# The last two chunks of the first feed-forward: four and four feature tiles become two and six, and the last chunk's down weights are split into other buffers

## The chip, the cores and the metric

The kernel runs on one core of one Trainium2 chip. The metric is the time of one execution in device microseconds (us). All operands are 32-bit; products are computed in three passes on numbers split into a high and a low part.

## The reference, cut to what matters

One decoder layer on 512 tokens of width 1024. Three sub-layers follow each other, each between two RMS norms:

```python
h = h + 0.5 * rmsnorm(swiglu(rmsnorm(h, ffn1_pre_w), ffn1_w_gu, ffn1_w_down), ffn1_post_w)
u = rmsnorm(h, mix_pre_w)
h = h + rmsnorm(token_mixing(u, mem, w_in, ...), mix_post_w)
h = h + 0.5 * rmsnorm(swiglu(rmsnorm(h, ffn2_pre_w), ffn2_w_gu, ffn2_w_down), ffn2_post_w)

def swiglu(x, w_gu, w_down):
    g, u = split(x @ w_gu, 2)          # 1024 x 5632, two halves of 2816
    return (silu(g) * u) @ w_down      # 2816 x 1024
```

The 2816 hidden features are 22 tiles of 128. The token mixing begins with a projection of the normed tokens `u` by parts of `w_in`.

## The kernel before, in words

**Splitting.** A 32-bit operand is split by `split` (L160): ScalarE (ACT) writes the high part (L161), VectorE (DVE) writes the rest (L162, through `tt`, so its rows show L158). A product is then three matmuls: hi by hi, hi by lo, lo by hi. `mm3` (L339) issues them with 512 moving columns (L341 to L343), `product` (L355) with 256 columns (L361 to L363).

**Gate and up.** For the feature tiles 2 to 21 a gate tile and an up tile are computed together as a pair, by seven products instead of eight on quarter blocks of the tokens and the weights (`pair`, L366): products 1, 6, 5, 7, 2, 3, 4 in this order, each of 4 x 3 matmuls of 256 columns. The moving operands of products 1, 2 and 3 are quarters of the split tokens `xhi`/`xlo`. Those of products 4, 5, 6 and 7 are combinations of token quarters, stored split in four tile pairs that the code calls `t4`, `t1`, `t2` and `t3` (`self.xc`, L80, and the table `self.xop`, L83). Each is a high and a low tile of 128 x 4 x 256. They are written by `prenorm` (L234 to L238) for the tokens of the next sub-layer, when the third and the fourth token tile are normed, and are read by every pair until the sub-layer's last pair. The seven weight operands of a pair are split into the pool `w` (18 buffers of 128 x 512, so nine split operands), in the order of the products.

**Down.** The features go in chunks, `CHUNKS1` and `CHUNKS2` (L44, L45): 2, 4, 4, 4, 4, 4 tiles. While the pairs of one chunk are computed, the down projection of the chunk before is woven in: eight accumulations `down` (four token tiles by two column halves, L462), spread over the chunk's pairs (L501). Each has 3 matmuls of 512 columns for each feature tile of the chunk, and ends in one VectorE addition to `y`. Its weights are split into the pool of 37 general buffers `slots` (`down_weights`, L457).

**The last chunk.** It has no pairs to be woven into. Its down weights are loaded row by row of tiles (L508, 512 KB each, into the pool `st` of four buffers) and split at L509: the tiles 0 to 2 into the pool `w`, the fourth (`j >= 3`) into `slots`. Then, for each of the four token tiles (L513), come two accumulations, the second one of the fourth token tile in two parts of 256 columns; squares (L174), the reciprocal root on GpSimd (POOL, L181), the products with the gain, the addition to the residual (`postnorm`, L244). A task is spawned (L527) that norms the token tile for the next sub-layer: squares, reciprocal root, `u` (L190), eight TensorE transposes into PSUM (L196), splits into `xhi`/`xlo` (L217), copies (L208), and the combinations for the third and fourth tile. The task gives way after `u` and is resumed when a count of TensorE time (`tick`, L109) has grown by `LAT['norm'] = 8` us; that sets where its transposes stand in TensorE's instruction stream.

**What follows.** The mixing begins with `values` (L847): eight split weight operands in the pool `w` (`rows`, L274), and four accumulations of 24 matmuls of 512 columns, one for each token tile, each of which needs its token tile normed. Three pairs follow. A scheduler orders each engine's instructions when the kernel is built: it goes by the order in which they were written and by when it takes their operands to be ready. Every engine then runs its list in that order.

The second feed-forward is the same function, with `CHUNKS2`.

Of the kernel before, what the change touches and what calls it, by code (L numbers as in the profile page):

```python
# [40 lines left out]

ORDER = ("hg0", "prep", "v1", "hg1", "v2", "kv", "v0", "dil0", "mq0", "mq1", "dil1", "b_hg", "b_mem", "b_dil")

CHUNKS1 = (2, 4, 4, 4, 4, 4)  # L44
CHUNKS2 = (2, 4, 4, 4, 4, 4)  # L45

LAT = dict(comb=1.0, mem0=0.5, mem1=8.0, mem2=1.5, hg=1.5, hgx=6.0, hg1=6.0, hg2=11.0, hg3=6.0, hg4=6.0, dil0=4.0, dil1=17.0, dil2=5.0,
# [2 lines left out]
HALVES = (slice(0, 512), slice(512, 1024))  # L50


class Layer:
# [193 lines left out]
    def load(self, w, r0, nr, c0, ncol):  # L247

        st = self.stage.tile([P, nr, ncol], F32, tag="st", name=f"st{self.uid()}")
        self.bring(st, w.rearrange("(k p) c -> p k c", p=P)[:, r0:r0 + nr, c0:c0 + ncol])  # L250
        return st

    def unit(self, shape, slot=False):

        if slot:
            return self.slot(shape, F32R)
        return self.wpool.tile(list(shape), F32R, tag="w", name=f"w{self.uid()}")
# [163 lines left out]
    def ffn(self, w_gu, w_down, w_post, ready, reload, after, chunks, early, plain):  # L421
# [63 lines left out]
        f0, before, ws = 0, None, []  # L485
        for n in chunks:
            act = []
            for j in range(n):
                if before and 2 * j % n == 0:
                    ws = []  # L490
# [12 lines left out]
                        down(i % NT, i // NT, before[2], ws, before[0] == 0)  # L503
            before = (f0, n, act)
            f0 += n
        ws = []
        for j in range(n):
            st = self.load(w_down, before[0] + j, 1, 0, D)  # L508
            ws.append([self.wsplit(st[:, 0, HALVES[hf]], j >= 3) for hf in range(2)])  # L509
        h = reload()  # L510
        gain = self.bcast_gain(w_post)
        tasks = []
# [495 lines left out]
def layer_kernel(ctx, tc, a, nbias, hmask, out):  # L1008
# [35 lines left out]
    def reload(src):  # L1044
        def go():
            h = [[L.slot() for _ in range(2)] for _ in range(NT)]
            for t in range(NT):
                for hf in range(2):
                    L.fetch(h[t][hf], src(t, hf))
            return h  # L1050
        return go

    def follow(dest, w):

        gain, raw = [], {}

        def after(h, t):
            if t == 0:
                gain.extend(L.bcast_gain(w))
            for hf in range(2):  # L1060
                nc.sync.dma_start(out=dest[t][hf], in_=h[t][hf])
            return L.prenorm(h[t], gain, t, LAT['norm'], raw)
        return after

    def store(h, t):
        for c, n in ((0, 512), (512, 256), (768, 256)) if t == NT - 1 else ((0, 512), (512, 512)):
# [4 lines left out]
    ready = L.ffn(a["ffn1_w_gu"][0], a["ffn1_w_down"][0], a["ffn1_post_w"][0], [first, second],  # L1071
                  reload(lambda t, hf: x[t * P:(t + 1) * P, HALVES[hf]]), follow(h1, a["mix_pre_w"][0]), CHUNKS1, PLAN['early1'], PLAN['plain1'])
    z = L.mixing(a, ready, nbias)
# [44 lines left out]
```

## Time and profile before

| | us |
|---|---|
| median of 3 runs (lowest to highest) | 1367.3 (1366.92 to 1368.4) |
| the profiled execution | 1367.62 |
| its span, first to last instruction | 1365.8 |
| TensorE busy in it | 1331.6 |
| VectorE busy | 1050.7 |
| ScalarE busy | 742.2 |

The profile is that of one execution, and its times count from the start of the span. Engines are PE (TensorE), PEld (TensorE's weight loads), DVE (VectorE), ACT (ScalarE), POOL (GpSimd) and SP (the queue that issues most DMAs). A row of the timeline has the start, the duration, the engine, the line, the operation, the output and inputs by the program's names, and in square brackets the idle time before the instruction and what ended it. Matmuls overlap: the time that one costs is the distance between two starts, not its duration. Buffers of one pool share a name: `w` is the split-weight pool, `s` the general slots, `st` the staged loads, `ps` and `px` PSUM.

### The profile page before, as it was taken

To read this page: it belongs to the slowest core of one execution; us is meant where nothing else is said; L and a number is where in the kernel's file an instruction comes from. 1 tells how busy PE (TensorE), PEld (TensorE's weight loads), DVE (VectorE), ACT (ScalarE), POOL (GpSimd) and SP (SyncE) were. 2 spreads that over 40 slices of the span, in tenths; PEclk is the share of its full clock that TensorE was granted. 3 is DMA by queue.
4 is the path that set the end of the run, shared out by engine and by line. 5 is a ranking of instruction groups with operands and counts; after the bars stand their busy time and mean duration, and the time that the engine had idled before them with its cause. 6 is when DMAs were issued, how large, how long until landed. Compare 5 with 4: busy or idle time off the path is not lost.

```text
span 1365.8 us, 24324 instructions
## 1 busy us (share of the span) xinstructions
PE 1331.6 (97%) x9197; PEld 1233.0 (90%) x9197; DVE 1050.7 (77%) x1996; ACT 742.2 (54%) x1527; POOL 107.0 (8%) x140
## 2 busy tenths in 40 slices
PE   6999999999999999999999999999999999999997
PEld 6999999999789888899899999999889999999996
DVE  6887776777798975598888988897478877677765
ACT  6665544555467655355554755566366655445541
POOL 1111111110100000000000100000011111111100
PEclk9999999999999999999999999999999999999999
DMA  9676565554435335334224333335465765655513
GB/s 271 141 182 184 148 156 142 143 151 125 168 94 177 96 98 163 123 102 117 63 78 124 100 95 93 108 94 154 135 190 135 186 181 151 152 139 148 146 47 139
DMA packets 238123, 185.76 MB, mean 136 GB/s; under 512 B 9109, under 2 KB 198966, under 8 KB 238006
## 3 DMA queue, kind: packets, MB, share of 16 engines
q1 hardware_dynamic: 224246, 160.02, 39.5%
q0 software_dynamic: 12032, 21.04, 9.4%
q10 hardware_dynamic: 1728, 3.15, 0.6%
q8 instruction: 72, 1.18, 0.3%
q14 instruction: 45, 0.37, 0.1%
HBM read 153.73 MB, written 9.47 MB: 119 GB/s over the span
## 4 chain that ended last, share of the span: by engine, by line
PE 87%; DVE 6%; issue 3%; DMA 2%; ACT 1%; POOL 1%; SPq 0%; POOLq 0%; DVEq 0%; ACTq 0%
PE ps L361 17%; PE ps L363 17%; PE ps L362 17%; PE ps L341 6%; PE ps L342 6%; PE ps L343 6%; PE px L341 5%; PE px L342 5%; PE px L343 5%; PE px L348 4%; DVE s L158 2%; PE px L352 1%; DVE w L158 1%; POOL r L181 1%; DVE s L244 1%
## 5 line engine op out<-in xcount | busy, mean ns | idle before, releaser
L161 ACT ACTIVATE w<-sum 128x512 fp32r<-128x512 f32 x288 | 180.2, 631 | 215.9 <-PE ps L362 180.3
L158 DVE TENSOR_TENSOR w<-sum,w 128x512 fp32r<-128x512 f32 x288 | 196.9, 687 | 76.9 <-ACT w L161 75.9
L361 PE MATMUL ps<-xhi,w 128*128 128x256 f32 x864 | 246.3, 285 | 0.9 <-ACT s L379 0.9
L363 PE MATMUL ps<-xhi,w 128*128 128x256 f32 x864 | 244.8, 283 | 0.0
L362 PE MATMUL ps<-xlo,w 128*128 128x256 f32 x864 | 244.4, 283 | 0.0
L161 ACT ACTIVATE w<-st 128x512 fp32r<-128x512 f32 x260 | 162.9, 630 | 126.7 <-PE ps L362 90.0
L158 DVE TENSOR_TENSOR w<-st,w 128x512 fp32r<-128x512 f32 x260 | 177.2, 688 | 39.3 <-ACT w L161 37.9
L158 DVE TENSOR_TENSOR s<-s,s 128x256 f32<-128x256 f32 (+3 forms) x316 | 176.8, 564 | 16.2 <-ACT s L161 4.6
L361 PEld LDWEIGHTS ps<-xhi,w 128*128 128x128 f32 x864 | 165.6, 192 | 3.8 <-ACT s L379 1.2
L362 PEld LDWEIGHTS ps<-xlo,w 128*128 128x128 f32 x864 | 165.6, 192 | 2.4 <-issue 0.2
L363 PEld LDWEIGHTS ps<-xhi,w 128*128 128x128 f32 x864 | 165.5, 192 | 0.0
L158 DVE TENSOR_TENSOR sum<-sum,st 128x512 f32<-128x512 f32 x176 | 120.4, 687 | 10.9 <-issue 5.0
L158 DVE TENSOR_TENSOR s<-s,ps 128x256 f32<-128x256 f32 (+1 forms) x194 | 92.3, 476 | 29.4 <-PE ps L343 24.0
L341 PE MATMUL px<-s,s 128*128 128x512 f32 x288 | 112.6, 391 | 0.0
L342 PE MATMUL px<-s,s 128*128 128x512 f32 x288 | 112.5, 391 | 0.0
L343 PE MATMUL px<-s,s 128*128 128x512 f32 x288 | 112.0, 389 | 0.0
L361 PE MATMUL ps<-t4hi,w 128*128 128x256 f32 x288 | 81.9, 284 | 0.8 <-ACT s L382 0.8
L361 PE MATMUL ps<-t3hi,w 128*128 128x256 f32 x288 | 82.6, 287 | 0.0
L362 PE MATMUL ps<-t3lo,w 128*128 128x256 f32 x288 | 82.0, 285 | 0.0
L361 PE MATMUL ps<-t1hi,w 128*128 128x256 f32 x288 | 81.7, 284 | 0.0
L363 PE MATMUL ps<-t1hi,w 128*128 128x256 f32 x288 | 81.6, 283 | 0.0
L362 PE MATMUL ps<-t2lo,w 128*128 128x256 f32 x288 | 81.5, 283 | 0.0
(186 smaller groups left out, 3344.2 us busy)
## 6 DMA issues: line engine op xcount, KB each, us to landing
st<-in_ffn_w_gu_dram SPq DMA_DIRECT2D x48, 512.0 KB, 4.9
st<-in_w_in_dram SPq DMA_DIRECT2D x48, 512.0 KB, 3.7
st<-in_ffn_w_down_dram SPq DMA_DIRECT2D x44, 512.0 KB, 3.8
sum<-in_ffn_w_gu_dram SPq DMA_DIRECT2D x80, 256.0 KB, 3.4
sh<-in_ffn_w_gu_dram SPq DMA_DIRECT2D x40, 256.0 KB, 3.8
sum<-sh POOLq DMA_DIRECT2D x40, 256.0 KB, 3.6
sum<-st POOLq DMA_DIRECT2D x40, 256.0 KB, 3.3
sum<-in_w_in_dram SPq DMA_DIRECT2D x32, 256.0 KB, 2.9
```

The lines of the kernel that those rows point to most:

```text
L158: self.pin(self.nc.vector.tensor_tensor(out=out, in0=a, in1=b, op=op))
L161: self.pin(self.nc.scalar.activation(hi, src, AF.Copy))
L181: self.nc.gpsimd.tensor_tensor(out=r, in0=v, in1=self.mhalf[:, :1], op=ALU.pow)
L244: self.nc.vector.scalar_tensor_tensor(out=h[hf][:, cs], in0=y[hf][:, cs], scalar=r, in1=h[hf][:, cs], op0=ALU.mult, op1=ALU.add)
L341: mm(out, lhsT=lhs[0], rhs=rhs[0], start=first, stop=False)
L342: mm(out, lhsT=lhs[0], rhs=rhs[1], start=False, stop=False)
L343: mm(out, lhsT=lhs[1], rhs=rhs[0], start=False, stop=last)
L348: self.nc.tensor.matmul(out, lhsT=lhsT, rhs=rhs, start=start, stop=stop, **k)
L352: self.nc.tensor.transpose(out, in_, self.ident)
L361: mm(out, lhsT=lh, rhs=rh, start=first and k == 0, stop=False, skip_group_check=True)
L362: mm(out, lhsT=lh, rhs=rl, start=False, stop=False, skip_group_check=True)
L363: mm(out, lhsT=ll, rhs=rh, start=False, stop=k == 3, skip_group_check=True)
```

## The change

The chunks of the first feed-forward become 2, 4, 4, 4, 2, 6; those of the second stay. In both, the weights of the last chunk go elsewhere: tiles 0 and 1 into the pool `w` as before, the others into the space of the combinations `t2`, `t1`, `t3`, `t4`, in this order, each cut into two pieces of 128 x 512. With six tiles that is 8 of the 12 split operands, column half 0 in `t2` and `t1`, half 1 in `t3` and `t4`; with four tiles it is 4 of 8, in `t2` and `t1`. None of them go to `slots` any more.

```diff
-CHUNKS1 = (2, 4, 4, 4, 4, 4)
+CHUNKS1 = (2, 4, 4, 4, 2, 6)
 CHUNKS2 = (2, 4, 4, 4, 4, 4)
...
+    def spare(self):
+
+        for n in ("t2", "t1", "t3", "t4"):
+            for j in range(2):
+                yield [x[:, 2 * j:2 * j + 2, :].rearrange("p a b -> p (a b)") for x in self.xc[n]]
...
-        ws = []
+
+        ws, spare = [], list(self.spare())
         for j in range(n):
             st = self.load(w_down, before[0] + j, 1, 0, D)
-            ws.append([self.wsplit(st[:, 0, HALVES[hf]], j >= 3) for hf in range(2)])
+            ws.append([])
+            for hf in range(2):
+                i = j - 2 + (n - 2) * hf
+                if j < 2 or i >= len(spare):
+                    ws[-1].append(self.wsplit(st[:, 0, HALVES[hf]]))
+                else:
+                    self.split(*spare[i], st[:, 0, HALVES[hf]])
+                    ws[-1].append(spare[i])
```

## The prediction

> **What bounds the kernel now.** I read the page first, then the windows around the edited code, then TensorE's waits there and the timeline of each engine.
>
> ```profile
> span 1365.8 us, 24324 instructions
> PE 1331.6 (97%) x9197; PEld 1233.0 (90%) x9197; DVE 1050.7 (77%) x1996; ACT 742.2 (54%) x1527; POOL 107.0 (8%) x140
> PE 87%; DVE 6%; issue 3%; DMA 2%; ACT 1%; POOL 1%; SPq 0%; POOLq 0%; DVEq 0%; ACTq 0%
> ```
>
> TensorE is busy 97% of the span and is 87% of the chain that ended last. So an edit pays only where TensorE stands still. These windows are four pairs of the first feed-forward, its last chunk up to the last down matmul, the values stage, and the three pairs after it:
>
> ```profile
> 193.71:255.87 62.16, 62.16 (x435) 58.33 (x434) 45.94 (x81) 31.08 (x60) 6.98 (x8) 1.00 0.60 152
> 345.50:371.10 25.60, 24.47 (x126) 20.30 (x125) 18.04 (x32) 10.43 (x27) 3.70 (x5) 1.00 0.48 167
> 371.10:398.10 27.00, 24.36 (x113) 19.14 (x112) 25.71 (x48) 18.89 (x41) 2.86 (x5) 1.00 0.32 99
> 398.10:428.30 30.20, 30.20 (x253) 30.20 (x252) 28.04 (x53) 20.66 (x43) 0.00 (x0) 1.00 0.53 152
> ```
>
> The columns are window, length, then busy time and count of PE, PEld, DVE, ACT, POOL, then granted clock and DMA share. Pairs run without a hole; the last chunk and the values stage do not, and in the values stage DVE is busy 25.71 of 27.00 us. TensorE's own starts show each hole:
>
> ```profile
> 345.49 0.39 PE L341 MATMUL ps<-w,s 128*128 128x512 f32 x1
> ...
> 359.54 0.39 PE L343 MATMUL ps<-w,s 128*128 128x512 f32 x1
> 359.84 1.32 PE L352 MATMUL px<-ident,s 128*128 128x128 f32 x8
> 360.92 0.48 PE L341 MATMUL ps<-w,s 128*128 128x512 f32 x1
> ...
> 365.57 0.39 PE L343 MATMUL ps<-s,s 128*128 128x512 f32 x1
> 367.08 0.66 PE L352 MATMUL px<-ident,s 128*128 128x128 f32 x4 [1.13 <-DVE s L190]
> ...
> 370.89 0.40 PE L341 MATMUL ps<-w,xhi 128*128 128x512 f32 x1
> ...
> 373.86 0.39 PE L341 MATMUL ps<-w,xhi 128*128 128x512 f32 x1
> 375.02 0.63 PE L352 MATMUL px<-ident,s 128*128 128x128 f32 x4 [0.77 <-DVE s L190]
> ...
> 378.95 0.39 PE L342 MATMUL ps<-w,xhi 128*128 128x512 f32 x1
> 381.11 0.50 PE L342 MATMUL ps<-w,xhi 128*128 128x512 f32 x1 [1.78 <-DVE w L158]
> ...
> 383.29 0.39 PE L341 MATMUL ps<-w,xhi 128*128 128x512 f32 x1
> 383.74 1.29 PE L352 MATMUL px<-ident,s 128*128 128x128 f32 x8
> ...
> 398.07 0.28 PE L361 MATMUL ps<-xhi,w 128*128 128x256 f32 x1
> ```
>
> From 345.49 to 359.54 there are 62 steps of 512-column matmuls, 14.05/62 = 0.227 us each. A 256-column step is 30.20/253 = 0.119 us. A hole is a start, minus the start before it, minus 0.227: 0.07, 1.28, 0.93, 1.93 and 0.22 us, together 4.43. Three sorts of wait are in them: for `u` (L190) of a token tile that TensorE is to transpose, 0.07 + 1.28 + 0.93 + 0.22 = 2.50; and for a split weight of the values stage, 1.93. The same from above: the last chunk's 84 whole and 24 half-width matmuls, 96 of the values stage and 32 transposes (eight cost 360.92 − 359.84 = 1.08) need 180 x 0.227 + 24 x 0.119 + 4 x 1.08 = 48.0 of the 398.07 − 345.49 = 52.6 us. About 4.5 us is all that the edited place can give.
>
> **Why the holes are there.** A token tile takes TensorE 24 x 0.227 = 5.4 us, and its transposes stand 8 us of TensorE time behind its end. Tile 0 ended at 345.5 + 5.4 = 350.9, tile 1 at 356.4.
>
> ```profile
> 351.13 0.69 DVE L158 TENSOR_TENSOR s<-s,ps 128x512 f32<-128x512 f32 x1 [2.03 <-PE ps L343]
> 353.51 0.69 DVE L158 TENSOR_TENSOR s<-s,s 128x512 f32<-128x512 f32 x1 [0.69 <-DMA s<-in_ffn_post_w_dram]
> ...
> 359.03 1.42 DVE L190 SCALAR_TENSOR_TENSOR s<-s,r,s 128x512 f32<-128x512 f32 x2 [0.44 <-POOL r L181]
> ...
> 361.57 0.20 DVE L180 TENSOR_SCALAR v<-ss,ss 128x1 f32<-128x1 f32 x1
> ...
> 366.28 1.42 DVE L190 SCALAR_TENSOR_TENSOR s<-s,r,s 128x512 f32<-128x512 f32 x2
> ```
>
> Tile 0's chain, alone, has the first half of `u` after 359.84 − 350.9 = 8.9 us, 0.7 of them for a gain that landed late. Tile 1's needs 367.08 − 356.4 = 10.7: its second addition and its `v` (361.57) stand behind tile 0's `u` on DVE. DVE falls behind because four chains of about 7.6 us each (ten steps of 0.6 to 0.7, two of 0.2 and two waits of 0.44 for POOL) meet a period of 5.4.
>
> **The change, part by part.** *A longer period.* With six tiles a token tile takes 36 x 0.227 = 8.2 us. DVE's 7.6 us fit, barely. TensorE reaches the transposes of tile 0 at 8.2 + 0.7 = 8.8 us behind its end, as now, and those of tiles 1 and 2 at 9.9 and 10.2 (eight transposes of the tile before lie between). Readiness is 8.2 to 8.9 alone, plus up to 1.4 for the L190 pair of the tile before: 9.6. So the holes of 1.28 and 0.93 close. For tile 3 nothing about the place changes, 8 us behind, 38 x 0.227 + 1.08 = 9.7; the shortest chain is 8.9 and it still meets tile 2's splits and combinations. I leave 0.8 there (bounds 0.3 and 1.8).
>
> *The pool `w`.* The last chunk held 12 of its 18 buffers, now 8.
>
> ```profile
> 331.46 0.63 ACT L161 ACTIVATE w<-st 128x512 fp32r<-128x512 f32 x1 [4.89 <-PE ps L362]
> ...
> 337.22 0.63 ACT L161 ACTIVATE w<-st 128x512 fp32r<-128x512 f32 x1 [0.55 <-PE ps L362]
> ...
> 340.10 0.63 ACT L161 ACTIVATE w<-st 128x512 fp32r<-128x512 f32 x1 [0.17 <-PE ps L362]
> ...
> 364.90 0.61 ACT L161 ACTIVATE w<-st 128x512 fp32r<-128x512 f32 x1
> ...
> 376.38 0.62 ACT L161 ACTIVATE w<-st 128x512 fp32r<-128x512 f32 x1
> ...
> 380.32 0.61 ACT L161 ACTIVATE w<-st 128x512 fp32r<-128x512 f32 x1
> ```
>
> Now three of the eight operands of the values stage (337.22 to 340.10) are split before the last chunk, into buffers that the last pair gives back; a fourth at 364.9; the rest from 376.38 on, because their buffers hold down weights until the last down matmul at 370.8. In the new order five come from the last pair, a sixth when token tile 3 begins, two near its end. The hole of 1.93 shrinks to about 0.2 (bounds 0 and 1). DVE also loses some 3 x 0.6 us of work from its fullest stretch.
>
> *The new wait.* These rows are the end of the last pair (its next TensorE work starts at 340.02), the low part of its activation, and the first later write of a combination:
>
> ```profile
> 340.02 0.40 PE L341 MATMUL px<-s,s 128*128 128x512 f32 x1
> ...
> 342.14 0.69 DVE L158 TENSOR_TENSOR s<-s,s 128x512 fp32r<-128x512 f32 x1
> ...
> 386.69 0.63 ACT L161 ACTIVATE t1hi<-s 128x512 fp32r<-128x512 f32 x1 [0.51 <-DVE s L158]
> ```
>
> The eight splits into `t2`, `t1`, `t3`, `t4` wait for products 6, 5, 7 and 4 of the last pair. Behind them on ACT stand that pair's copies, silu and split, and DVE's halves wait for ACT. The last pair ends, two short downs follow (12 x 0.227 = 2.7 us), then the last chunk begins with the `w` tiles 0 and 1; half 0 of the last tile is needed 15 x 0.227 = 3.4 us later and comes from `t1`, free two products and more before the end. Half 1 in `t4` is needed 4.1 + 2.7 us in. Slack is over 3 us everywhere; cost nothing. The combinations' next writers come 386.7 − 370.9 = 15.8 us after the last down matmul now, so their wait is hidden too. The other cover is thinner: the gain's DMA, which stands in SP's order behind the residual's reload. It was 0.7 late and now has 2.8 us more, but the two woven downs before it are 2.7 us shorter; I charge 0.2 for it (bounds 0 and 2).
>
> *Two and six tiles.* All matmuls of the downs stay, eight additions a chunk too.
>
> ```profile
> L158 DVE TENSOR_TENSOR s<-s,px 128x512 f32<-128x512 f32 x8 | 5.5, 684 | 4.3 <-PE px L343 4.1
> L158 DVE TENSOR_TENSOR s<-st,s 128x512 fp32r<-128x512 f32 x8 | 5.1, 685 | 0.0
> ```
>
> Without these 10.6 us a pair costs DVE (45.94 − 10.6)/4 = 8.8 us. The six-tile chunk gives TensorE 6 x 84 x 0.119 + 48 x 0.227 = 70.9 us and DVE 6 x 8.8 + 5.5 + 2.6 = 60.9, 86%. In the window of three pairs DVE did 28.04 in 30.20, 93%, and TensorE had no hole. The two-tile chunk leaves more room than now. So nothing.
>
> *The rest.* Six more column-halved steps cost 6 x (2 x 0.119 − 0.227) = 0.1. The second feed-forward's last chunk changes only buffers; the list of TensorE's waits from 1280 us on is empty: nothing.
>
> Sum: of 4.43 there stay 0.8 + 0.2 + 0.2, and 0.1 comes on: 3.1 us saved. The profiled execution took 1367.62 (front table), 0.3 above the median, so 1364.5 for it and 1364.2 for the median. Behind the values stage TensorE runs solid, so the gain is carried on. Bounds: 4.4 − 0.3 − 0.1 = 4.0 at best; 4.4 − 1.8 − 1.0 − 0.3 − 0.1 = 1.2 at worst.
>
> **The rivals.** *DVE keeps the wait.* If the work behind the last down matmul, 25.71 us on DVE, is what sets tile 3, then only the split weights' hole goes, 1.9 − 0.1: 1365.5. For it: that window is 95% full. Against: the three weight splits from 376.38 on leave it, and whatever of tiles 1 and 2 is late now.
>
> *ACT's list blocks.* If the eight splits stand ahead of the last pair's silu and split, the activation comes 8 x 0.63 = 5.0 us later than now, when it is there 342.8 − 340.0 = 2.8 behind the pair's end: at 7.8, while it is needed at 2.7 + 3.4 = 6.1: 1.7 us lost, 1365.9. The row at 331.46 shows ACT standing 4.89 us at one such split. [...]
>
> *Slower: DVE bounds the six-tile chunk.* In order, with its waits for ACT and PSUM, DVE may not fill more than its mean of 77%: 60.9/0.77 = 79.1 instead of 70.9, 8.2 lost and 3.1 won, 1372.3. It decides below 60.9/(70.9 + 3.1) = 82%. Against it are the 93%; for it, that pairs here also wait for accumulating DMAs.
>
> **How the numbers follow.** Forecast 0.70, DVE keeps the wait 0.14, ACT blocks 0.06, slower 0.10. A change is told from none at 0.2%, 2.7 us. Of the forecast's range of 1.2 to 4.0, some four fifths lie beyond 2.7, as its middle does: faster 0.56. The rest of it and the two middle rivals are the same: 0.34. Slower 0.10. The range goes from 1362.9, a little below the best bound, to 1366.9, which leaves out the slower rival and little else.
>
> **What would show it.** Right: no wait of over 0.5 us of transposes for L190 of tiles 1 and 2; no wait for `w` in the values stage; first down matmul of the last chunk to first matmul of the first mixing pair about 52.6 + 10.9 − 3.1 = 60.4 us; DVE below 90% there; the six-tile chunk without a hole. Wrong: a hole at the last chunk's first matmuls (a split late), a hole of over 2 us at tile 3's transposes, or pairs in the six-tile chunk farther apart than 11.8 us.

## The result and the profile after

| | before | after |
|---|---|---|
| median of 7 runs each (lowest to highest), us | 1368.4 (1366.85 to 1370.85) | 1362.52 (1360.14 to 1365.05) |
| the profiled execution, us | 1367.62 | 1360.29 |
| its span, us | 1365.8 | 1358.3 |

The ratio is 0.9946, with an interval from 0.9929 to 0.9962: faster by 5.9 us between the medians. The forecast was faster by 3.1 us (1364.2); the measured median lies 0.4 us below the lower end of its range. The direction and the place were right and the size was not. The rows of the changed kernel show two gains: 4.7 us where the prediction looked for 3.1, and 1.4 us at the end of the kernel, where it looked for nothing.

**The edited place.** TensorE's timeline of the changed kernel, with the first down matmul of the last chunk, the eight transposes of each token tile, the last down matmul, and the first matmul of the first mixing pair (the changed file's L347 to L349, L358 and L367 are L341 to L343, L352 and L361 of before):

```profile
333.59 0.39 PE L347 MATMUL ps<-w,s 128*128 128x512 f32 x1
...
350.60 1.03 PE L358 MATMUL px<-ident,s 128*128 128x128 f32 x8
351.39 0.47 PE L347 MATMUL ps<-w,s 128*128 128x512 f32 x1
...
358.75 0.39 PE L349 MATMUL ps<-t4hi,s 128*128 128x512 f32 x1
359.15 1.38 PE L358 MATMUL px<-ident,s 128*128 128x128 f32 x8
360.28 0.48 PE L347 MATMUL ps<-w,s 128*128 128x512 f32 x1
...
368.67 0.28 PE L349 MATMUL ps<-t4hi,s 128*128 128x256 f32 x1
...
369.49 1.03 PE L358 MATMUL px<-ident,s 128*128 128x128 f32 x8
...
377.63 0.40 PE L349 MATMUL ps<-w,xlo 128*128 128x512 f32 x1
377.87 1.03 PE L358 MATMUL px<-ident,s 128*128 128x128 f32 x8
...
392.37 0.28 PE L367 MATMUL ps<-xhi,w 128*128 128x256 f32 x1
```

From the chunk's first matmul to the first mixing pair it is 392.37 − 333.59 = 58.78 us; below, this is "the stretch". Before it was 52.58. The two more feature tiles put 48 steps of 0.2266 us (14.05/62, from the prediction), 10.88 us, more of matmuls into it, so the stretch of before with all its holes would be 63.46: 4.7 us were saved. The prediction named 60.4 as the sign. No row of transposes carries a bracket any more. Eight transposes that wait for nothing take 351.39 − 350.60 = 0.79 us. What is left of the waits is at tile 1: 359.15 − 358.75 − 0.23 = 0.17 us ahead of its transposes, and 360.28 − 359.15 − 0.79 = 0.34 inside them, 0.5 together. The windows of the chunk, of the values stage and of the first pairs (columns as before):

```profile
333.60:369.70 36.10, 36.00 (x184) 30.25 (x183) 27.98 (x50) 18.30 (x45) 3.93 (x6) 1.00 0.59 201
369.70:390.00 20.30, 20.30 (x99) 17.02 (x98) 18.34 (x35) 11.80 (x25) 2.31 (x4) 1.00 0.16 53
390.00:420.20 30.20, 30.20 (x245) 29.77 (x243) 27.12 (x50) 20.66 (x41) 0.00 (x0) 1.00 0.48 140
```

TensorE is busy without a hole in the values stage too. TensorE's waits from the second pair of the first feed-forward to the mixing pairs are one line, a wait near the start of the kernel:

```profile
PE ps L367 <- ACT s L388: 0.8, 1, 0.8
```

In the 118.60 us up to the last chunk's first matmul (215.00 to 333.60) TensorE is busy for 118.60 and VectorE for 90.70. So the six-tile chunk's pairs stood nowhere, the last chunk began without a wait, and no split weight was late.

**The end of the kernel.** TensorE's last matmul starts at 1356.52 us before and at 1350.40 after. From there to the end of the span it is 1365.8 − 1356.52 = 9.28 us before and 1358.3 − 1350.40 = 7.90 after. In that time VectorE works off the token tiles. Its rows in the kernel before, from the residual's addition (L244) of the second token tile to that of the third:

```profile
1349.18 1.42 DVE L244 SCALAR_TENSOR_TENSOR s<-s,r,s 128x512 f32<-128x512 f32 x2 [0.44 <-POOL r L181]
1350.52 0.68 DVE L158 TENSOR_TENSOR s<-s,ps 128x512 f32<-128x512 f32 x1
1351.98 0.69 DVE L158 TENSOR_TENSOR s<-s,s 128x512 f32<-128x512 f32 x1 [0.79 <-ACT s L174]
1352.59 0.68 DVE L158 TENSOR_TENSOR s<-s,ps 128x512 f32<-128x512 f32 x1
1354.07 0.21 DVE L180 TENSOR_SCALAR v<-ss,ss 128x1 f32<-128x1 f32 x1 [0.79 <-ACT s L174]
...
1355.32 1.42 DVE L244 SCALAR_TENSOR_TENSOR s<-s,r,s 128x512 f32<-128x512 f32 x2 [0.44 <-POOL r L181]
```

and in the changed kernel:

```profile
1343.14 1.41 DVE L244 SCALAR_TENSOR_TENSOR s<-s,r,s 128x512 f32<-128x512 f32 x2 [0.44 <-POOL r L181]
1344.47 1.34 DVE L158 TENSOR_TENSOR s<-s,ps 128x512 f32<-128x512 f32 x2
1345.94 0.69 DVE L158 TENSOR_TENSOR s<-s,s 128x512 f32<-128x512 f32 x1
1346.61 0.21 DVE L180 TENSOR_SCALAR v<-ss,ss 128x1 f32<-128x1 f32 x1
...
1347.86 1.41 DVE L244 SCALAR_TENSOR_TENSOR s<-s,r,s 128x512 f32<-128x512 f32 x2 [0.45 <-POOL r L181]
```

Before, the product with the gain (the second row, `s<-s,s`) stands between the two additions from PSUM, and VectorE waits twice for a square on ScalarE, 0.79 us each. After, the two additions stand together, the squares run beside the product, and neither wait is there. From one L244 to the next it is 6.14 us before and 4.72 after: 1.42 us. The instructions are the same; the order in VectorE's built list is not.

Of the difference of the two spans, 7.5 us, 4.7 and 1.4 lie in these two places. The remaining 1.4 lies at the start (1.0) and in the long middle, from the first mixing pair to the last matmul (958.4 us before, 958.0 after). A part of that size differs between executions of one and the same kernel: a second execution of the changed kernel took 959.7 us for its middle.

### The profile page after: what moved, and what is told of

Same layout as the page of the kernel before. It is cut to its first block, busy times and chain, and to the rows that moved or that the text cites. A ratio compares the mean times of both kernels' runs of the same rounds, so it can differ in the third digit from the quotient of the medians.

```text
span 1358.3 us, 24350 instructions
## 1 busy us (share of the span) xinstructions
PE 1329.5 (98%) x9203; PEld 1232.7 (91%) x9203; DVE 1049.3 (77%) x1996; ACT 742.4 (55%) x1527; POOL 107.0 (8%) x140
## 4 chain that ended last, share of the span: by engine, by line
PE 87%; DVE 5%; issue 3%; DMA 2%; ACT 2%; POOL 1%; SPq 0%; DVEq 0%; POOLq 0%; ACTq 0%
PE ps L367 16%; PE ps L369 16%; PE ps L368 16%; PE ps L347 7%; PE ps L348 7%; PE ps L349 6%; PE px L347 4%; PE px L348 4%; PE px L349 4%; PE px L354 4%; PE px L358 2%; DVE s L158 1%; DVE w L158 1%; POOL r L181 1%; DMA sum<-sh 1%
## 5 line engine op out<-in xcount | busy, mean ns | idle before, releaser
L367 PE MATMUL ps<-xhi,w 128*128 128x256 f32 x864 | 246.2, 285 | 1.0 <-ACT s L385 1.0
L158 DVE TENSOR_TENSOR w<-st,w 128x512 fp32r<-128x512 f32 x256 | 174.2, 688 | 33.9 <-ACT w L161 32.1
L367 PEld LDWEIGHTS ps<-xhi,w 128*128 128x128 f32 x864 | 165.5, 192 | 4.0 <-ACT s L385 1.5
L347 PE MATMUL px<-s,s 128*128 128x512 f32 x272 | 106.3, 391 | 0.0
L348 PE MATMUL px<-s,s 128*128 128x512 f32 x272 | 106.3, 391 | 0.0
L349 PE MATMUL px<-s,s 128*128 128x512 f32 x272 | 105.8, 389 | 0.0
L367 PE MATMUL ps<-t4hi,w 128*128 128x256 f32 x288 | 81.9, 284 | 0.8 <-ACT s L388 0.8
L367 PE MATMUL ps<-t3hi,w 128*128 128x256 f32 x288 | 82.5, 287 | 0.0
L367 PE MATMUL ps<-t1hi,w 128*128 128x256 f32 x288 | 81.8, 284 | 0.0
L369 PE MATMUL ps<-t3hi,w 128*128 128x256 f32 x288 | 81.5, 283 | 0.0
```

Of the source, the lines that this page charges most:

```text
L158: self.pin(self.nc.vector.tensor_tensor(out=out, in0=a, in1=b, op=op))
L347: mm(out, lhsT=lhs[0], rhs=rhs[0], start=first, stop=False)
L348: mm(out, lhsT=lhs[0], rhs=rhs[1], start=False, stop=False)
L349: mm(out, lhsT=lhs[1], rhs=rhs[0], start=False, stop=last)
L367: mm(out, lhsT=lh, rhs=rh, start=first and k == 0, stop=False, skip_group_check=True)
L369: mm(out, lhsT=ll, rhs=rh, start=False, stop=k == 3, skip_group_check=True)
```

## The experiments

Two numbers are read from each profile: the stretch, and the end (from the last matmul's start to the end of the span). The ratio is to the kernel before, on the same chip.

| kernel | stretch, us | end, us | ratio (interval) |
|---|---|---|---|
| before | 52.58 | 9.28 | |
| after | 58.78 | 7.90 | 0.9946 (0.9929 to 0.9962) |
| after, once more | 58.86 | 7.84 | 0.9962 (0.9950 to 0.9974) |
| new buffers, chunks of before | 51.62 | 7.82 | 0.9994 (0.9982 to 1.0006) |
| six tiles, `w` held as before | 58.72 | 7.91 | 0.9969 (0.9958 to 0.9981) |
| change in the first feed-forward alone | 58.61 | 9.40 | 0.9968 (0.9957 to 0.9980) |
| chunks 2, 4, 4, 2, 4, 6 | 59.30 | 7.83 | 0.9972 (0.9960 to 0.9984) |
| two idle VectorE passes a tile | 59.39 | 7.88 | 0.9960 (0.9946 to 0.9973) |
| two passes on the tile's chain | 62.10 | 7.91 | 0.9979 (0.9960 to 0.9998) |
| before, transposes placed at 10 us | 52.31 | 9.37 | 0.9999 (0.9983 to 1.0016) |
| before, no `slots` in the second feed-forward's last chunk | 53.77 | 7.93 | 1.0000 (0.9988 to 1.0012) |
| before, gain loaded first | 52.23 | 9.34 | 1.0005 (0.9993 to 1.0017) |
| two and six tiles in both | 58.29 | 7.40 | 0.9958 (0.9946 to 0.9970) |
| the same, once more | 58.64 | 7.39 | 0.9960 (0.9946 to 0.9974) |

A stretch of a kernel with a six-tile last chunk compares with 63.46, that of one with four with 52.58. A span is printed to 0.1 us, so an end is good to 0.05.

The two columns and the ratio do not always agree. "Six tiles, `w` held as before" should have 0.9955 by its rows (6.1 us) and "chunks 2, 4, 4, 2, 4, 6" 0.9959 (5.6 us); the one lies outside its measured interval, the other just outside, and both kernels gained some 1.8 us less than their rows give. The first one's profiled execution shows no loss in the two places, but a middle of 961.0 us. Whether that belongs to these kernels or to the execution stays open: two other kernels whose matmul lists behind the stretch are those of before as far as the second feed-forward's last chunk, "before, no `slots`" and "before, gain loaded first", had middles of 961.2 and 957.9 us. What follows rests on the rows of the two places.

### Which half of the edit closes which hole

**The buffers without the six tiles.**

```diff
-CHUNKS1 = (2, 4, 4, 4, 2, 6)
+CHUNKS1 = (2, 4, 4, 4, 4, 4)
```

> The chunks of before (4 and 4), the buffers of after: the last chunk of either feed-forward holds 8 split-weight buffers, not 12, and no slots. A token tile keeps its period of 5.4 us. Theory (two holes with two causes, and a third gain at the end): the hole for a split weight (1.93 us) goes, the holes for u (2.5 us) stay, so from the first down matmul of the last chunk to the first matmul of the first mixing pair about 50.7 us (52.6 before); behind the last matmul 7.9 us as after (9.3 before). In all 3.3 us off, ratio about 0.9976. Rival A (the pool alone did it: the late weight splits are what crowds VectorE): all holes go, 48 us, ratio 0.9955. Rival B (the longer period alone did it): 52.6 us, ratio 0.999.

The stretch got 1.0 us shorter. TensorE's waits from the last chunk to the mixing pairs in the kernel before:

```profile
PE px L352 <- DVE s L190: 1.9, 2, 1.1
PE ps L342 <- DVE w L158: 1.8, 1, 1.8
```

and with the new buffers alone:

```profile
PE px L358 <- DVE s L190: 2.6, 2, 1.5
PE ps L348 <- DVE w L158: 0.2, 1, 0.2
```

The wait for a split weight shrinks from 1.8 to 0.2, as the prediction had it for the pool; the waits for `u` grow from 1.9 to 2.6. Freeing the buffers moves most of the loss and does not remove it.

**The six tiles with the pool `w` as full as before.**

```diff
-                i = j - 2 + (n - 2) * hf
-                if j < 2 or i >= len(spare):
+                k = 3 if n == 6 else 2
+                i = j - k + (n - k) * hf
+                if j < k or i >= len(spare):
```

> The chunks of after (2 and 6), but in the first feed-forward the tiles 0 to 2 go into the split-weight pool (12 of its 18 buffers held, as before) and six of the eight spare pieces are used. Theory: the longer period of 8.2 us keeps the holes for u closed, the hole for a split weight comes back with 1 to 1.9 us: 59.8 to 60.7 us from the first down matmul of the last chunk to the first mixing pair (58.8 after); with the end of after, 4.2 to 5.1 us off in all, ratio 0.9963 to 0.9969. Rival A (the pool alone): the holes for u come back too, over 62.5 us, ratio above 0.998. Rival B (the period alone): 58.8 us, ratio 0.9955.

Here the last chunk holds 12 buffers of `w` again. The stretch is 58.72, as in the changed kernel, and in the values stage there is no wait for a weight; the 1 to 1.9 us expected there did not come. With the first experiment this makes a table of two by two: with four tiles there are waits whether 12 or 8 buffers are held, with six there is none of over 0.5 us in either case. By these rows the longer period of a token tile does it alone; the emptier pool is neither needed for it nor enough.

**The change in the first feed-forward alone.**

```diff
-                if j < 2 or i >= len(spare):
+                if n == 4:
+                    ws[-1].append(self.wsplit(st[:, 0, HALVES[hf]], j >= 3))
+                elif j < 2 or i >= len(spare):
```

> After, but the second feed-forward places its last chunk's weights as before. Theory: the end of the kernel is a part of the gain of its own: VectorE's list there is that of before again, 9.3 us from the last matmul to the end (7.9 after), everything ahead of it as after (58.8 us in the edited place): 4.7 us off in all, ratio about 0.9966. Rival (the shorter end was chance of one execution): 7.9 us or anything between, ratio as after.

The stretch is 58.61, and the end is back at 9.40. The place of the second feed-forward's weights, which the prediction had at nothing, is what makes the end shorter. The ratio, 0.9968, is that of 4.8 us less on 1367.6 (0.9965).

**Two, four and six.**

```diff
-CHUNKS1 = (2, 4, 4, 4, 2, 6)
+CHUNKS1 = (2, 4, 4, 2, 4, 6)
```

> Chunks 2, 4, 4, 2, 4, 6: the last chunk is six tiles long, the one before it four. Theory: only the last chunk's length and buffers matter, and the pairs hide all woven work: 58.8 us in the edited place, 7.9 us at the end, the time of after (ratio 0.9955), no hole in the pairs. Rival (the short chunk ahead of the last matters, for its free slots or its early reload): more holes than after in the last chunk, 1 us or more longer.

The six-tile chunk's pairs now carry the downs of four tiles, not of two. The stretch is 59.30, with one wait of 0.6 us for `u` before transposes. The two-tile chunk need not stand right before the last; what it costs to have it elsewhere is within 0.5 us by the rows.

### What is short in the last chunk: VectorE's time or a token tile's chain

**Two more passes off the chain.**

```diff
+            if not second:
+                for _ in range(2):
+                    self.tt(y[t][0], y[t][0], y[t][0], ALU.max)
             self.tt(y[t][0], y[t][0], gain[0], ALU.mult)
```

> After, with two more VectorE passes of 128x512 (about 0.6 us each) in each token tile of the first feed-forward's last chunk, ahead of the gain product; they leave the values as they are. Theory (VectorE's 7.6 us for a token tile just fit the period of 8.2): with 8.8 us it falls behind again and every chain is 1.2 us longer, holes for u of 2 to 4 us in all come back, so 61 to 63 us from the first down matmul of the last chunk to the first mixing pair (58.8 after). Rival (there is ample room, the holes went for another reason): under 59.4 us.

Eight passes of 0.6 us, some 4.9 us of VectorE's time, made the stretch only 59.39 − 58.78 = 0.6 us longer; 2 us and more were expected. The row of the window over the stretch in the changed kernel, and then in this one:

```profile
333.59:392.37 58.78, 58.68 (x292) 49.21 (x290) 48.69 (x86) 32.48 (x74) 6.25 (x10) 1.00 0.42 143
```

```profile
333.35:392.74 59.39, 58.84 (x292) 49.11 (x291) 53.92 (x96) 32.72 (x74) 6.25 (x10) 1.00 0.43 145
```

VectorE's busy time (the sixth number, its count behind it) rises by 5.2 us, from 83 to 91% (the count rises by ten, the eight passes and two more instructions that fall into the window), and TensorE hardly stands. The one wait that comes is for a split weight of the values stage, 0.5 us, with only 8 buffers of the pool held: with more work on VectorE a weight can be late although the pool is emptier. The prediction's "7.6 us fit, barely" was too dark: there was room for 1.2 us more in each token tile. In the first token tile both passes fall into times in which VectorE stood in the changed kernel (0.79 us for a square, 0.95 us for the gain).

**The same two passes on the chain**, between the second addition and the square of its sum:

```diff
+                    if not second and hf == 1 and cs.stop == 512:
+                        for _ in range(2):
+                            self.tt(y[t][1], y[t][1], y[t][1], ALU.max)
                     ss.append(self.square(y[t][hf][:, cs], hf, 0.5))
```

> The changed kernel, with two more 128x512 passes of VectorE for each token tile of the first feed-forward's last chunk, between the second addition and what reads its sum; they take the maximum of the sum with itself, so no value changes. Some 1.2 us for each token tile, and now on the chain from the down projection to the transposes. Theory A (in the six-tile chunk the transposes are only just in time, and the latency of a token tile's chain is what bounds it): waits of about 1 us before the transposes of at least two of the tiles, and 60.5 to 62.5 us from the chunk's first matmul to the first mixing pair, where the changed kernel has 58.8 us. Theory B (there is more than 1 us to spare in the chain too, as there was for passes off it): under 59.5 us, no wait over 0.5 us.

The stretch is 62.10: 3.3 us longer than in the changed kernel for the same work on VectorE, 2.4 of them in two holes ahead of transposes:

```profile
361.07 1.38 PE L358 MATMUL px<-ident,s 128*128 128x128 f32 x8 [1.17 <-DVE s L190]
371.53 1.29 PE L358 MATMUL px<-ident,s 128*128 128x128 f32 x8
381.25 1.29 PE L358 MATMUL px<-ident,s 128*128 128x128 f32 x8 [0.92 <-DVE s L190]
```

Of the gain of 6.1 us, 2.8 are left, a ratio of 0.9980 where 0.9979 was measured. So in the six-tile chunk, with its transposes 8 us behind, it is the length of a token tile's chain that has nothing to spare (tile 1 is 0.5 us late already without the passes), and not VectorE's time.

**The kernel before with the transposes placed later.**

```diff
-            return L.prenorm(h[t], gain, t, LAT['norm'], raw)
+            return L.prenorm(h[t], gain, t, 10.0 if dest is h1 else LAT['norm'], raw)
```

> The kernel before, with one number changed: the transposes and mixing norms behind the first feed-forward are placed 10 us of TensorE time behind a tile's end, not 8 us. The last chunk stays at four feature tiles, a token tile every 5.4 us of TensorE. Theory A (VectorE's queue is behind in this chunk, because a period of 5.4 us is shorter than its work of a token tile): the transposes wait as before or the wait moves to whatever TensorE reaches in their place; from the chunk's first matmul to the first mixing pair 51.5 to 52.6 us (before 52.58), the time within 0.1% of before. Theory B (the transposes were only placed too near the end of their token tile): the three waits for the transposed tiles, 2.4 us, close, that stretch takes 50.0 to 50.4 us, and the time is 0.1 to 0.2% under before, so that half of the gain of the six-tile chunk was to be had without it.

With the four-tile chunk of before, the first transposes stand 360.65 − 344.32 = 16.3 us behind the chunk's first matmul instead of 359.84 − 345.49 = 14.4, and the stretch is 52.31. The waits in the same part:

```profile
PE ps L342 <- DVE w L158: 2.0, 2, 1.8
PE px L352 <- DVE s L190: 1.1, 1, 1.1
PE ps L343 <- DVE xlo L158: 0.7, 1, 0.7
```

One wait for `u` went, and one for a low part of the tokens came. Placing the transposes 2 us later, in front of the same queue on VectorE, does not help: at 5.4 us a token tile the work is late at both places tried.

### What makes the end shorter

**The kernel before, with the second feed-forward's last weights all in the pool `w`.**

```diff
-            ws.append([self.wsplit(st[:, 0, HALVES[hf]], j >= 3) for hf in range(2)])
+            ws.append([self.wsplit(st[:, 0, HALVES[hf]], j >= (4 if second else 3)) for hf in range(2)])
```

> Before, with one edit: in the second feed-forward the last chunk's fourth tile is split into the split-weight pool too (16 of 18 buffers) and not into general slots. Nothing changes in the first feed-forward. Theory (the end is shorter because the four slots left free change VectorE's list: for the third token tile the second addition stands ahead of the first half's gain product): the end is that of after, 7.9 us from the last matmul (9.3 before), the edited place of the first feed-forward as before (52.6 us): 1.4 us off, ratio about 0.999. Rival (the spare space itself, or an earlier free weight, shortens the end): 9.3 us, ratio 1.

The combinations' space is not used, only the four buffers of `slots` are left free, and the end is 7.93. (The stretch is 53.77 in this execution, not the 52.6 expected; the mean granted TensorE clock of the whole execution was 0.993, in the kernel before 0.998, and the edit changes no list that early.) VectorE's rows there have the two additions together, as after:

```profile
1356.72 1.41 DVE L244 SCALAR_TENSOR_TENSOR s<-s,r,s 128x512 f32<-128x512 f32 x2 [0.45 <-POOL r L181]
1358.05 1.33 DVE L158 TENSOR_TENSOR s<-s,ps 128x512 f32<-128x512 f32 x2
1359.53 0.69 DVE L158 TENSOR_TENSOR s<-s,s 128x512 f32<-128x512 f32 x1
1360.18 0.21 DVE L180 TENSOR_SCALAR v<-ss,ss 128x1 f32<-128x1 f32 x1
```

**The kernel before, with the gain's load ahead of the residual's.**

```diff
+        if second:
+            gain = self.bcast_gain(w_post)
+            h = reload()
+        else:
+            h = reload()
+            gain = self.bcast_gain(w_post)
```

> Before, with one edit: in the second feed-forward the gain is loaded ahead of the residual, so it is there early too, but VectorE's list for the third token tile stays that of before (first addition, gain product, second addition). Theory (the order of that list is the cause): the end stays at 9.3 us, ratio about 1. Rival (the early gain is the cause): 7.9 us, ratio 0.999.

The end is 9.34, as before, with the product still between the additions. The gain's load is issued 24.4 us ahead of the last matmul here, 20.6 before and 22.6 after. So an early gain is not the cause by itself. What the free slots do is seen on the queue that loads the residual, first in the kernel before, then after:

```profile
1332.13 3.69 SPq L141 DMA_DIRECT2D s<-h  x8
1335.88 0.91 SPq L141 DMA_DIRECT2D s<-in_ffn_post_w_dram  x2
```

```profile
1310.48 17.32 SPq L141 DMA_DIRECT2D s<-h  x8
1327.85 0.90 SPq L141 DMA_DIRECT2D s<-in_ffn_post_w_dram  x2
```

The residual goes into `slots`. With four more of them free the first of its eight loads is issued 1350.40 − 1310.48 = 39.9 us ahead of the last matmul instead of 1356.52 − 1332.13 = 24.4, so 15.5 us earlier; the last is issued by 22.6 us ahead instead of 20.7, only 1.9 us earlier. And the built list of VectorE comes out in the other order. That freeing the slots changes the order, the runs show, and that the end goes with it: with the two additions together it is 7.8 to 7.9 us in every kernel with a four-tile last chunk there, with the product between them 9.3 to 9.4. No run changed the order alone, and which of the scheduler's estimates tips it was not tried. The 1.4 us are read from rows: from that chunk's first matmul to its last it is 21.79 us in all of these kernels, so nothing is paid there for the shorter end. The medians of the kernel without `slots` there and of the kernel before do not resolve a gain of 0.1% (the interval reaches from 0.9988 to 1.0012).

### The two sources, and the best version

**The changed kernel once more**, without an edit, in the same rounds as the last kernel below.

> The changed kernel once more, to see whether the two sources that the rows show (4.7 us around the first feed-forward's last chunk, 1.4 us at the end of the kernel) are the whole of its gain. Theory A (they are; what differs at the start of the kernel and in the middle differs from execution to execution): 6.1 us, a ratio of 0.9955 to the kernel before, within 0.0012; from the last matmul's start to the end 7.9 us, from the chunk's first matmul to the first mixing pair 58.8 us. Theory B (the 1.0 us less at the start and some more in the middle belong to the change): 7 us or more, 0.9949 or less. By the prediction's sum it would be 0.9977.

0.9962, and 0.9946 the first time; 6.1 us would be 0.9955, which lies in both intervals. The prediction's 0.9977 lies in neither. That the start and the middle belong to the change is not borne out: in the two profiled executions of this one kernel, the second feed-forward up to its last chunk took 290.44 and 292.11 us.

**Two and six tiles in both feed-forwards.**

```diff
-CHUNKS2 = (2, 4, 4, 4, 4, 4)
+CHUNKS2 = (2, 4, 4, 4, 2, 6)
```

> After, with chunks 2, 4, 4, 4, 2, 6 in the second feed-forward too. Theory: TensorE has no hole there to close, so the 2 and 6 cost and give nothing in the pairs; at the end VectorE is not behind, so the half-width addition follows the last matmul at once and the end is about 0.7 us shorter than after's 7.9. 6.8 us off before in all, ratio about 0.9950. Rival (two and six have a price of their own, hidden in after by the gain): the pairs of the second feed-forward show holes, or 1 us and more is lost from its first woven down to its last matmul: ratio 0.996 or above.

> Two and six feature tiles in both feed-forwards, on the same chip and in the same rounds as the changed kernel, which has them in the first alone. Theory A (the second feed-forward's last chunk had no hole, so only its order of work at the end can gain): 0.5 us shorter from the last matmul's start to the end, 7.4 us, the time within 1 us of the changed kernel, not to be told from it. Theory B (the longer period helps there too): 2 us or more under the changed kernel.

By the rows this is the best version: the end is 7.40 us, another 0.5 less, at a stretch of 58.29 and 58.64. The times do not tell it from the changed kernel: 1361.25 (1359.88 to 1364.79) beside 1361.81 (1361.46 to 1363.15) in the same rounds. There was no hole for a longer period to close in the second feed-forward.

## Why the prediction was wrong in size

- *TensorE bounds the kernel, and the place to gain is these holes*: right (TensorE is busy 97% of the span before and 98% after, and 4.7 us came from there). **"About 4.5 us is all that the edited place can give"** was too low. It priced eight transposes at 1.08 us from tile 0 of before; without a wait they take 0.79, so that tile, and tile 3 with 1.04, hid 0.3 more of a hole inside their transposes (the split ones of tiles 1 and 2 took 0.78 and 0.74). With 0.79, the prediction's own count gives 180 x 0.227 + 24 x 0.119 + 4 x 0.79 = 46.9 us for the stretch of before and 5.7 us above it. The same count for the changed kernel (222 x 0.227 + 36 x 0.119 + 4 x 0.79 = 57.8) leaves 0.9, of which some 0.5 is its wait at tile 1 and some 0.5 small gaps of under 0.1 us. So 5.2 of the 5.7 could go. (The prediction speaks of three sorts of wait and names two; the rows show no third.)
- *The longer period closes the holes of tiles 1 and 2*: right, and shown by the two-by-two. The sum for readiness, up to 9.6 us behind a tile's end, was close; the place was not. It put TensorE at the transposes of tile 1 9.9 us behind, eight transposes later than at those of tile 0. But `tick` counts transposes too, and without a wait TensorE would have been there 358.75 + 0.23 − 349.92 = 9.1 us behind the tile's end (its last matmul starts at 349.69). That is where 0.5 us stayed.
- **"For tile 3 ... I leave 0.8 there (bounds 0.3 and 1.8)"**: this step failed too. It took the shortest chain to be 8.9 us, the one of tile 0, and tile 3's to meet tile 2's work. The rows of VectorE after show otherwise:

```profile
368.30 1.42 DVE L190 SCALAR_TENSOR_TENSOR s<-s,r,s 128x512 f32<-128x512 f32 x2 [0.40 <-POOL r L181]
369.63 0.69 DVE L158 TENSOR_TENSOR w<-st,w 128x512 fp32r<-128x512 f32 x1
370.24 0.42 DVE L158 TENSOR_TENSOR s<-s,ps 128x256 f32<-128x256 f32 x1
...
376.39 1.42 DVE L190 SCALAR_TENSOR_TENSOR s<-s,r,s 128x512 f32<-128x512 f32 x2 [0.45 <-POOL r L181]
```

Tile 2's `u` is begun at 368.30, before TensorE's last down matmul (368.67). Tile 3 then has VectorE almost to itself, and its own `u` starts 376.39 − 368.67 = 7.7 us behind that matmul. The same two rows of the kernel before:

```profile
374.12 1.41 DVE L190 SCALAR_TENSOR_TENSOR s<-s,r,s 128x512 f32<-128x512 f32 x2 [0.40 <-POOL r L181]
...
382.84 1.42 DVE L190 SCALAR_TENSOR_TENSOR s<-s,r,s 128x512 f32<-128x512 f32 x2 [0.44 <-POOL r L181]
```

There the last down matmul started at 370.77; tile 2's `u` began 3.4 us behind it, and tile 3's 12.1 us. The estimate for tile 3 had kept tile 2's lateness, which the same edit removes. The other two remainders did not come: no wait for a weight, and for the gain VectorE stood 0.95 us (0.69 before), but tile 0's transposes followed the matmul ahead of them without a hole. So the sum "of 4.43 there stay 0.8 + 0.2 + 0.2" should have been 5.2 less 0.5: the ceiling was 0.8 too low and the remainders 0.7 too high, which but for 0.1 is the difference of 4.7 and 3.1.

- **"The second feed-forward's last chunk changes only buffers; the list of TensorE's waits from 1280 us on is empty: nothing"**: the third step that failed, by 1.4 us. The list is empty because the time lies behind TensorE's last matmul, where VectorE sets the end; and the buffers decide when the residual is loaded and in which order VectorE's list is built.
- *The weights' hole closes because the pool holds 8, not 12*: right as far as it goes (0.2 of 1.8 was left with that alone), but the pool was not the whole cause, since the six tiles close it with 12 held as well. The high part of the late weight, which the prediction shows, was there at 376.38 + 0.62 = 377.00 us; its low part began 3.4 us later, with six other instructions of VectorE in between:

```profile
380.37 0.68 DVE L158 TENSOR_TENSOR w<-st,w 128x512 fp32r<-128x512 f32 x1
```

So this hole, too, stood in part behind VectorE's list.

- *Two and six tiles cost nothing; the new wait costs nothing*: right. Of ScalarE's eight splits into the combinations the first and the last start at 323.13 and 331.38, ahead of the chunk's first matmul at 333.59, and cost TensorE nothing.
- *The rivals.* None came. VectorE did not bound the six-tile chunk (TensorE had no hole in the 118.60 us ahead of the last chunk), ScalarE's list did not block (copies and the silu stand among the eight splits, and no wait of ScalarE from 322 to 334 us is over 0.9), and VectorE did not keep its wait (0.5 us was left, at tile 1). What was missing was a case on the gaining side: the bound of 4.0 stood on the ceiling of 4.43 and on leftovers that never came to nothing together, and the end of the kernel had no bound at all. So the range ended too high. On the other side, the bound at worst took 0.3 for the gain, where its own bound was 2.

## What to carry to other kernels

Whether work hides behind a pipeline is read from the period against the chain of one item and its order in the queue, not from a busy share: VectorE was 83% busy in this stretch before (43.72 of 52.58 us) and after (48.69 of 58.78), with some 5 us of waits and with half a microsecond of them. When an edit removes the lateness of one item, cost the next item without that lateness too. And an edit that "changes only buffers" can move the issue of a load (here by 15.5 us) and, where a list is ordered at build time, turn the order of instructions far away; look behind the bounding engine's last instruction, where its list of waits shows nothing.

## What was not expected of the hardware

Two executions of one kernel differ at a single wait by as much as the change is worth at the end of the kernel. TensorE's largest wait in the start of the second feed-forward was 0.3 us in one execution of the changed kernel and 1.7 in the other:

```profile
PE ps L367 <- ACT s L385: 0.3, 1, 0.3
```

```profile
PE ps L367 <- ACT s L378: 1.7, 1, 1.7
```

In the start of the first feed-forward (50 to 100 us) the waits of over 0.4 us left holes of 1.8 us in the changed kernel, 2.0 in the kernel before, and 4.3 in the kernel with the new buffers alone, whose lists are those of before up to the last chunk. The kernel before without `slots` in the second feed-forward's last chunk, with the lists of before up to there, had one wait of 4.1 us. What makes these waits vary was not tried. It is why a gain of 1.4 us is read here from the rows of its place and not from a difference of two medians.
